# Attention stage: where the rounds of a top-k, a broadcast and the weight loads stand in their engines' orders

## The chip, the cores and the metric

The kernel runs on one core of one Trainium2 chip. The metric is the device time of one execution in microseconds. A core has five engines that run their own instruction queues in order: TensorE (PE: matmuls, and PEld for the loads of their weights), VectorE (DVE), ScalarE (ACT), GpSimd (POOL) and SyncE (SP), which here only issues DMAs. Weights and data come from HBM to SBUF by DMA; matmul results land in PSUM, in banks of 512 floats per partition.

## The reference: one step of a two-layer encoder

The input is 512 new frames of one stream ("prompt") and 64 further frames of another ("sample"), 576 tokens in all, of width 1024. Layer 0 mixes tokens with causal pooling, layer 1 with sparse attention; each layer then has an MLP of width 4096 with squared ReLU, and RMS norms stand before each part and at the end. The change touches layer 1's attention:

```python
p = h @ w_in                       # q (16 heads x 64), k, v (4 x 64), qi (8 x 64), ki (64), wi (8)
q, k, qi, ki = rope(q), rope(k), rope(qi), rope(ki)
logits = einsum('bthd,bsd->bths', qi, kidx) * 64 ** -0.5
score  = einsum('bths,bth->bts', relu(logits), wi)          # the indexer
score  = where(kpos // 64 <= qpos // 64, score, NEG)
_, idx = top_k(score, n_sel)                                # 128 of 512, 144 of 576
s = (q . k[idx]) * 64 ** -0.5                               # only the selected keys
o = softmax(s) @ v[idx];  y = o @ w_o
```

All arithmetic is in 32 bits. The kernel keeps each operand as a rounded part and a rest and adds three products, so that one block of weights means three times the matmuls.

## The kernel before, in words

Data lie transposed, features on the 128 partitions and the 576 tokens along the free axis (the prompt's 512, then the sample's 64). Weights come in blocks of 128x1024 floats. `load` takes a raw buffer (`raw_tile`, line 139) and issues the DMA, on ScalarE's queue for the attention's weights and on SyncE's for most of the MLP's; `split_block` (line 200) makes the rounded part on ScalarE (line 205) and the rest on VectorE (line 206) or GpSimd; three split blocks (`BLOCKS`) and two raw buffers (`RAWS`) exist. `loaded` (line 246) issues loads in the order of a list of jobs; `LOADS_AHEAD` says how many raw blocks may be held beyond the one that is being split: four where the stage has the extra raw buffers named `more`, one in the attention stage. `next_block` keeps `AHEAD`, two, split blocks ready.

The program is traced through a scheduler which, against a simulated timeline, chooses the order of each engine's instructions: of what is ready then, what was traced first goes first. The order is fixed before the run. `tc.manual_schedule(engines=...)` leaves the named engines' instructions in the order in which they are written; the kernel has two such places, outside the attention. `tc.issue_after(instruction)` keeps what is traced under it behind that instruction in its engine's order; `mixing` uses it for SyncE.

The attention stage, `attention` (line 1086), goes like this.

1. Two blocks of the indexer's queries, tokens 128 to 575, are projected (`project_qi`, line 1102, tile `pi`). Behind the first, `norm.stats` sums squares by matmul (tile `st`) and makes each token's factor `r` on VectorE (lines 394 to 401). `norm.spread` (line 350) then puts `r` on diagonals (lines 365 and 368), multiplies them by ones on TensorE (tile `rb`, line 355), so that each partition gets the factors of all tokens, and copies the two halves on ScalarE (line 356). With them the cosine table (GpSimd, line 1115) and the sine table (VectorE, line 1116) are scaled.
2. The block of the indexer's key and weights is projected (`ki`), and `rope` (line 1126) applies the tables. For the key, copies and products are done in two halves of 288 tokens (lines 1184 to 1190). The indexer's weights are transposed into the bank `pw` (line 1191), which comes from the pool `ps` (two tiles of two banks), and scaled (line 1195). The pool `po` has four tiles of one bank.
3. k, q and v are projected (tiles `pj` and `v`); the queries go through HBM (`qd`). Between the steps of these projections, `pace` (line 1421) puts `index_scores` (line 1211) of row blocks 1 to 3: 128 query tokens each, against i + 1 blocks of 128 keys. Row block 4 is the sample: 64 queries, 576 keys.
4. `top_k` (line 1247) works in place on a row block's scores `work[i]`: 16 rounds (18 in block 4), each of which finds the eight largest of each row (line 1253) and replaces them with a mark (line 1254). A last step (line 1257) makes a mask of it. All on VectorE.
5. `steps` (line 1394) runs 40 units of attention, each two heads (four for the sample) of one key head and one row block: units 0 to 15 take blocks 0 and 1 in turn, 16 to 23 block 2, 24 to 31 block 3, 32 to 39 block 4. A unit has scores on TensorE (`sc`, lines 1289 and 1297), a masked reduction on VectorE (line 1268, with the row's extreme `nm`), an exponential on ScalarE (line 1269), transposes on TensorE (`pt`, line 1309), a copy (line 1310) and the product with the values (`o`, line 1328). `top_k(i)` is traced ahead of the first unit of block i.
6. From unit 18 on, a first part of the output projection (`wa`, line 1383) goes between the units, and the rest (`wo`) behind them.

Of the kernel before, what the change touches and what calls it, by code (L numbers as in the profile page):

```python
# [16 lines left out]
P = 128  # L17
# [23 lines left out]
LOADS_AHEAD = {True: 4, False: 1}  # L41
# [4 lines left out]
STATS = (3, 0)  # L46
BLOCKS = 3
# [4 lines left out]
def pool_dsa_kernel(ctx: ExitStack, tc: tile.TileContext, a, o):  # L52
# [86 lines left out]
    def raw_tile(mlp=False):  # L139
        more = False  # L140
        if mlp and "more" in phase:
            t, turns["raw"] = turns["raw"], turns["raw"] + 1
            more = t % 4 > 1
        return (phase["more"] if more else raws).tile([P, 4 * 264], F32, tag="raw", name=uid("raw"))

    def load(src, n, queue, mlp=False):
        raw = raw_tile(mlp)
        d = queue.dma_start(raw[:, :n], src)
        if queue is nc.sync:
            last_of["sync"] = d  # L150
        return raw
# [94 lines left out]
    def loaded():  # L246

        waiting, held = [], 0
        while jobs or waiting:
            while jobs and held < LOADS_AHEAD["more" in phase] and ("last" in phase or jobs[0][0] not in ("pair", "made")):  # L250
# [67 lines left out]
    def project(pt, w, xs, between=iter(()), cols=((0, HT), (HT, HT)), ks=range(KT)):  # L318

        for k in ks:  # L320
            next(between, None)
            wh, wl = at(w, k)
            for i, (wt, part) in enumerate(((wh, 0), (wh, 1), (wl, 0))):
                for h, (c, m) in enumerate(cols):
                    pe.matmul(  # L325
                        pt[h][:, :m] if isinstance(pt, tuple) else pt[:, h, :m], wt, xs[k][:, part, c:c + m],
                        start=(k == ks[0] and i == 0), stop=(k == ks[-1] and i == 2),
# [758 lines left out]
    def attention(parts):  # L1086
# [15 lines left out]
        def project_qi():  # L1102
            pt = psum1("pi")
            project((pt,), next_block(), xs, cols=((P, T - P),))
            return pt[:, :T - P]

        q0 = [project_qi()]
        norm.stats()
        r = norm.r
        q0.append(project_qi())  # L1110
        two = psum("rb")
        rb = norm.spread((two[:, 0], two[:, 1]))
        pki = psum("ki")
        project(pki, next_block(), xs)
        pool.tensor_tensor(cs, cs, rb, ALU.mult)
        dve.tensor_tensor(sn, sn, rb, ALU.mult)
        def split_cache(src, s, new, sub=dve):
# [3 lines left out]
            raw = raw_tile()  # L1121
# [62 lines left out]
        for h in range(2):  # L1184
            at = slice(h * HT, (h + 1) * HT)
            act.copy(wt[0:32, at], pki[0:32, h, :HT])
            for to, c, table in ((t1, 96, cs), (t2, 64, sn)):
                for i in range(2):
                    rows = slice(c, c + 32) if i == 0 else slice(160 - c, 192 - c)
                    dve.tensor_tensor(to[32 * i:32 * i + 32, at], pki[rows, h, :HT], table[rows, at], ALU.mult)  # L1190
        pw = psum("pw")[:, 0]
# [55 lines left out]
        def top_k(i):  # L1247
# [3 lines left out]
            for _ in range(16 if i < 4 else 18):  # L1251
                m8 = small(8, "m8")
                dve.max(m8[:np_], wk[:np_])  # L1253
# [333 lines left out]
```

## Time and profile before

| | |
|---|---|
| median of 3 runs | 1120.38 us (1119.23 to 1123.69) |
| the profiled execution | 1120.8 us |
| its span | 1119.0 us |
| mean granted TensorE clock | 0.986 |
| the attention stage in the trace | 433 us to some 726 us |
| DMA, whole span | 183.54 MB, 164 GB/s |

Times in the trace count from the start of the span. A row of the timeline has start, duration, engine, line, operation, output and inputs, shapes and count; in brackets stands how long the engine had been idle and what released it. A row of waits has the waiting engine and its line, whom it waited for, the total in us, how often, and the longest. A round of the top-k shows as MAX8, MATCH_VALUE_LOAD and MATCH_REPLACE8. Rows of MAX8 can be told apart by their width: 256, 384 and 512 for row blocks 1 to 3, 64x576 for block 4.

### The profile page before, as it was taken

How to read it: one execution, taken by the hardware profiler on the slowest of the kernel's cores; microseconds unless marked ns; L12 is line 12 of the kernel's file. 1: busy time of each engine (PE TensorE's matmuls, PEld its weight loads, DVE VectorE, ACT ScalarE, POOL GpSimd, SP SyncE). 2: the span in 40 equal slices, each digit the busy share in tenths (PEclk: the TensorE clock that was granted, in tenths of full speed). 3: DMA queues.
4: the chain of work that ended last, by engine and by line, in shares of the span. 5: the costliest groups of instructions: out<-in, count | busy, mean ns of one | idle time of the engine just before them, and what ended most of it. 6: DMA issues, size and time to landing. Idle time of an engine off the chain costs nothing.

```text
span 1119.0 us, 20356 instructions
## 1 busy us (share of the span) xinstructions
PE 1083.9 (97%) x8027; PEld 1064.5 (95%) x8027; DVE 798.4 (71%) x1445; ACT 557.5 (50%) x940; POOL 296.5 (26%) x227
## 2 busy tenths in 40 slices
PE   9999999999999999999789999999999999999996
PEld 8999999999999989899778999999999999999995
DVE  7767656756755887789988963778757867865644
ACT  8544344334434454354358665655536636644542
POOL 3014504532451560287815342001000000000002
PEclk9999999999999999999969999999999999999998
DMA  6265489479568977476622333357576655545402
GB/s 221 70 192 139 140 237 272 122 203 274 154 163 254 241 185 227 116 217 169 177 86 57 108 98 108 109 174 211 166 227 179 194 169 162 162 160 171 142 19 85
DMA packets 81263, 183.54 MB, mean 164 GB/s; under 512 B 11809, under 2 KB 23376, under 8 KB 81168
## 3 DMA queue, kind: packets, MB, share of 16 engines
q1 hardware_dynamic: 64512, 143.94, 39.7%
q0 software_dynamic: 13056, 25.17, 13.6%
q10 hardware_dynamic: 3600, 13.14, 3.8%
q8 instruction: 63, 1.03, 0.4%
q14 instruction: 32, 0.26, 0.1%
HBM read 167.14 MB, written 61.22 MB: 204 GB/s over the span
## 4 chain that ended last, share of the span: by engine, by line
PE 72%; DVE 13%; DMA 5%; ACT 3%; POOL 3%; issue 3%; SPq 0%; DVEq 0%; ACTq 0%; POOLq 0%
PE up L586 17%; PE seed L428 15%; PE c L428 10%; PE a L428 10%; PE dn L325 4%; DVE w L206 4%; PE wo L325 2%; PE o L1328 2%; DMA mixed<-mixed 2%; DVE work L1254 2%; DVE m L1253 2%; PE wa L325 2%; PE pb L1053 1%; PE pi L325 1%; PE sc L1289 1%
## 5 line engine op out<-in xcount | busy, mean ns | idle before, releaser
L205 ACT CAST w<-raw 128x1024 fp32r<-128x1024 f32 (+2 forms) x242 | 211.2, 890 | 210.1 <-PE seed L428 80.5
L206 DVE TENSOR_TENSOR w<-raw,w 128x1024 fp32r<-128x1024 f32 (+2 forms) x224 | 249.1, 1119 | 50.0 <-ACT w L205 49.3
L586 PE MATMUL up<-xs,w 128*128 128x288 f32 x1536 | 206.3, 295 | 0.0
L586 PEld LDWEIGHTS up<-xs,w 128*128 128x128 f32 x1536 | 204.0, 188 | 0.2
L428 PE MATMUL seed<-u,w 128*128 128x288 f32 x1008 | 146.4, 296 | 3.0 <-ACT seed L447 1.4
L428 PEld LDWEIGHTS seed<-u,w 128*128 128x128 f32 x1008 | 138.1, 188 | 4.3 <-ACT seed L447 1.6
L428 PE MATMUL c<-u,w 128*128 128x288 f32 x672 | 100.8, 297 | 2.0 <-DVE w L206 1.2
L428 PE MATMUL a<-u,w 128*128 128x288 f32 x672 | 100.0, 295 | 1.5 <-ACT w L205 1.2
L428 PEld LDWEIGHTS c<-u,w 128*128 128x128 f32 x672 | 93.2, 188 | 3.2 <-DVE w L206 1.7
L428 PEld LDWEIGHTS a<-u,w 128*128 128x128 f32 x672 | 93.0, 188 | 2.3 <-ACT w L205 1.7
L811 POOL TENSOR_TENSOR x<-x,spare 128x320 f32<-128x320 f32 (+1 forms) x9 | 8.2, 946 | 233.3 <-ACT spare L807 233.3
L325 PE MATMUL pj<-xs,w 128*128 128x288 f32 x480 | 67.3, 295 | 2.3 <-DVE wi L1195 1.0
L325 PEld LDWEIGHTS pj<-xs,w 128*128 128x128 f32 x480 | 65.0, 188 | 3.7 <-issue 2.5
L235 POOL DMA_DIRECT2D mixed<-in_w_down x24 | 27.6, 1271 | 145.3 <-DMA mixed<-mixed 94.2
L235 POOL DMA_DIRECT2D mixed<-in_w_up x24 | 28.0, 1210 | 141.6 <-DMA mixed<-mixed 100.4
L428 PE MATMUL seed<-bx,w 128*128 128x288 f32 x432 | 62.5, 296 | 0.0
L428 PEld LDWEIGHTS seed<-bx,w 128*128 128x128 f32 x432 | 59.3, 188 | 0.1
L206 DVE TENSOR_TENSOR w<-sum,w 128x1024 fp32r<-128x1024 f32 (+1 forms) x32 | 34.6, 1080 | 34.5 <-ACT w L205 34.5
L284 POOL TENSOR_TENSOR sum<-raw 128x512 f32<-128x512 f32 x16 | 24.2, 1516 | 125.1 <-DMA raw<-in_w_down 125.1
L721 DVE SCALAR_TENSOR_TENSOR v<-up,rbm 128x288 f32<-128x288 f32 x80 | 32.6, 450 | 31.8 <-PE up L586 28.9
L205 ACT CAST w<-sum 128x1024 fp32r<-128x1024 f32 (+1 forms) x32 | 26.7, 834 | 56.6 <-POOL sum L289 45.2
L1269 ACT ACTIVATE p<-p,nm 128x128 f32<-128x128 f32 (+4 forms) x72 | 41.8, 582 | 20.2 <-DVE nm L1268 20.0
(298 smaller groups left out, 2047.8 us busy)
## 6 DMA issues: line engine op xcount, KB each, us to landing
raw<-in_w_up SPq DMA_DIRECT2D x52, 512.0 KB, 4.5
raw<-in_w_down SPq DMA_DIRECT2D x52, 512.0 KB, 4.4
raw<-mixed SPq DMA_DIRECT2D x48, 512.0 KB, 4.1
mixed<-in_w_down POOLq DMA_DIRECT2D x24, 512.0 KB, 8.3
mixed<-mixed SPq DMA_DIRECT2D x24, 512.0 KB, 8.2
mixed<-in_w_up POOLq DMA_DIRECT2D x24, 512.0 KB, 10.3
raw<-in_w_in ACTq DMA_DIRECT2D x15, 512.0 KB, 4.5
mixed<-in_w_down SPq DMA_DIRECT2D x12, 512.0 KB, 7.3
```

Source lines behind the costliest of these rows:

```text
L205: act.copy(w[:, 0, at], src[:, at])
L206: how["sub"].tensor_tensor(w[:, 1, at], src[:, at], f32(w[:, 0, at]), ALU.subtract)
L235: pool.dma_start(to, add, accum_op=ALU.add)
L284: pool.tensor_tensor(s[:, :512], r2[:, :512], r2[:, 512:], ALU.add)
L325: pe.matmul(pt[h][:, :m] if isinstance(pt, tuple) else pt[:, h, :m], wt, xs[k][:, part, c:c + m], start=(k == ks[0] and i == 0), stop=(k = ...
L428: pe.matmul(bank[:, :HT], wt[:, at], ut, start=first and j == 0 and i == 0, stop=j == 3 and i == 2, skip_group_check=True)
L586: pe.matmul(pt[h][:, :HT], w[:, wt, k * P:(k + 1) * P], moving(k, part, h), start=n == 0 and i == 0, stop=n == KT - 1 and i == 2)
L721: dve.scalar_tensor_tensor(v[:, 2 * i + h], pt[h][:, :HT], 0.0, halves(norm.rb)[:, h], ALU.max, ALU.mult)
L1253: dve.max(m8[:np_], wk[:np_])
L1254: dve.match_replace(wk[:np_], m8[:np_], wk[:np_], TAKEN)
L1269: act.activation(dst, dst, AF.Exp, scale=-1.0, bias=nm, accum_out=sums)
L1328: pe.matmul(oc[:, 2 * s + hh], pT[:, c:c + P], V[:, kt, vs], start=kt == 0, stop=kt == i)
```

## The change

It has five parts, all in the attention stage.

- `HELD` holds a round of the top-k and so all later rounds of its block, since each works on what the one before left: round 10 of block 2 is issued behind unit 1's last masked reduction, round 0 of block 3 behind unit 3's, round 0 of block 4 behind unit 9's.
- TensorE's instructions from the first `project_qi` to the key block are left in written order, and `norm.spread` stands amid the second block: behind six of its eight steps.
- A third raw buffer of 1024 columns, which every third load of at most 1024 columns takes; two raw blocks are held ahead rather than one.
- The copy and the products of the indexer's key take both halves in one instruction.
- The bank `pw` comes from the pool `po`.

```diff
+HELD = {(2, 10): 1, (3, 0): 3, (4, 0): 9}
...
+    def raw_tile(mlp=False, n=4 * 264):
+        for name, every in (("more", 4), ("third", 3)):
+            if name in phase and (mlp or name == "third" and n <= 1024):
+                turns["raw"] += 1
+                if turns["raw"] % every > 1:
+                    return phase[name].tile([P, 4 * 264 if name == "more" else 1024], F32, tag="raw", name=uid("raw"))
+        return raws.tile([P, 4 * 264], F32, tag="raw", name=uid("raw"))
...
-            while jobs and held < LOADS_AHEAD["more" in phase] and ("last" in phase or jobs[0][0] not in ("pair", "made")):
+            while jobs and held < (4 if "more" in phase else 2 if "third" in phase else 1) and ("last" in phase or jobs[0][0] not in ("pair", "made")):
...
-        def project_qi():
+        def project_qi(amid=None):
             pt = psum1("pi")
-            project((pt,), next_block(), xs, cols=((P, T - P),))
+            w = next_block()
+            for ks in (range(KT - 2), range(KT - 2, KT)) if amid else (range(KT),):
+                if ks[0]:
+                    amid()
+                project((pt,), w, xs, cols=((P, T - P),), ks=ks, ends=(0, KT - 1))
             return pt[:, :T - P]
 
-        q0 = [project_qi()]
-        norm.stats()
-        r = norm.r
-        q0.append(project_qi())
-        two = psum("rb")
-        rb = norm.spread((two[:, 0], two[:, 1]))
-        pki = psum("ki")
-        project(pki, next_block(), xs)
+        with tc.manual_schedule(engines={ENG.PE}):
+            q0 = [project_qi()]
+            norm.stats()
+            r = norm.r
+            two = psum("rb")
+            q0.append(project_qi(lambda: norm.spread((two[:, 0], two[:, 1]))))
+            rb = norm.rb
+            pki = psum("ki")
+            project(pki, next_block(), xs)
...
-        for h in range(2):
-            at = slice(h * HT, (h + 1) * HT)
-            act.copy(wt[0:32, at], pki[0:32, h, :HT])
-            for to, c, table in ((t1, 96, cs), (t2, 64, sn)):
-                for i in range(2):
-                    rows = slice(c, c + 32) if i == 0 else slice(160 - c, 192 - c)
-                    dve.tensor_tensor(to[32 * i:32 * i + 32, at], pki[rows, h, :HT], table[rows, at], ALU.mult)
-        pw = psum("pw")[:, 0]
+        act.copy(halves(wt[0:32]), pki[0:32, :, :HT])
+        for to, first, table in ((t1, 96, cs), (t2, 64, sn)):
+            for i, c in enumerate((first, 160 - first)):
+                dve.tensor_tensor(halves(to[32 * i:32 * i + 32]), pki[c:c + 32, :, :HT], halves(table[c:c + 32]), ALU.mult)
+        pw = psum1("pw")
...
-            for _ in range(16 if i < 4 else 18):
+            for n in range(16 if i < 4 else 18):
                 m8 = small(8, "m8")
-                dve.max(m8[:np_], wk[:np_])
+                behind = HELD.get((i, n))
+                with tc.issue_after(units[behind].softmax.ins) if behind else nullcontext():
+                    dve.max(m8[:np_], wk[:np_])
...
-    with stage(under=1, xs=1, slots=1, cst1=1, tmps=5, cst2=1), ExitStack() as parts:
+    with stage(under=1, xs=1, slots=1, cst1=1, tmps=5, cst2=1, third=1), ExitStack() as parts:
```

`softmax` now returns its reduction, which each unit keeps as `self.softmax`; `project` takes `ends`, the steps at which a bank's sum begins and ends, so that one sum can be written in two calls.

More of the change, by code (lines that the diff above doesn't have):

```diff
@@ L1 @@
-from contextlib import ExitStack, contextmanager
+from contextlib import ExitStack, contextmanager, nullcontext
 import numpy as np
@@ L40 @@
 RAWS = 2
-LOADS_AHEAD = {True: 4, False: 1}
 FACTORS = ("b11", "b22", "b21", "t3", "t1", "t2", "t4")
@@ L137, in pool_dsa_kernel @@
     last_of = {}
[L139 to L144, printed above, removed]
+    def raw_tile(mlp=False, n=4 * 264):
[5 more added lines that the diff above has]
+        return raws.tile([P, 4 * 264], F32, tag="raw", name=uid("raw"))
     def load(src, n, queue, mlp=False):
-        raw = raw_tile(mlp)
+        raw = raw_tile(mlp, n)
         d = queue.dma_start(raw[:, :n], src)
@@ L316, in split, with project @@
             dve.scalar_tensor_tensor(dst[:, 1], src, scale, f32(dst[:, 0]), ALU.mult, ALU.subtract)
-    def project(pt, w, xs, between=iter(()), cols=((0, HT), (HT, HT)), ks=range(KT)):
+    def project(pt, w, xs, between=iter(()), cols=((0, HT), (HT, HT)), ks=range(KT), ends=None):
         for k in ks:
@@ L326, in project @@
                         pt[h][:, :m] if isinstance(pt, tuple) else pt[:, h, :m], wt, xs[k][:, part, c:c + m],
-                        start=(k == ks[0] and i == 0), stop=(k == ks[-1] and i == 2),
+                        start=(k == (ends or ks)[0] and i == 0), stop=(k == (ends or ks)[-1] and i == 2),
                     )
@@ L1120, in split_cache @@
             dve.tensor_copy(t[:, :, TP:], f32(new[:, :, TP:]))
-            raw = raw_tile()
+            raw = raw_tile(n=TP)
             nc.sync.dma_start(raw[:, :TP], src)
@@ L1267, in softmax @@
             nm = small(1, "nm")
-            dve.tensor_tensor_reduce(dst, src, mask, -0.125, 3e38, ALU.add, ALU.min, nm)
+            d = dve.tensor_tensor_reduce(dst, src, mask, -0.125, 3e38, ALU.add, ALU.min, nm)
             act.activation(dst, dst, AF.Exp, scale=-1.0, bias=nm, accum_out=sums)
+            return d
         class Unit:
@@ L1290, in scores @@
                     for hh in range(2):
-                        softmax(pt[:, hh, :n], mask, self.pr[:, hh], self.group.sums[:, 2 * s + hh:2 * s + hh + 1])
+                        self.softmax = softmax(pt[:, hh, :n], mask, self.pr[:, hh], self.group.sums[:, 2 * s + hh:2 * s + hh + 1])
                 else:
@@ L1297, in scores @@
                             pe.matmul(pt[:, c, :HT], q[:, s], self.group.ck[:, part, c * HT:(c + 1) * HT], start=part == 0, stop=part == 1)
-                    softmax(pt[:, :, :HT], halves(mask), halves(self.pr), self.group.sums[:, s:s + 1])
+                    self.softmax = softmax(pt[:, :, :HT], halves(mask), halves(self.pr), self.group.sums[:, s:s + 1])
             def transpose(self):
```

## The prediction, made before the changed kernel was timed

> **What bounds the kernel now.** The page comes first: the span of the profiled execution, the engines, the clock.
>
> ```profile
> span 1119.0 us, 20356 instructions
> PE 1083.9 (97%) x8027; PEld 1064.5 (95%) x8027; DVE 798.4 (71%) x1445; ACT 557.5 (50%) x940; POOL 296.5 (26%) x227
> ```
>
> TensorE is busy 97% of the span, so nothing off it counts unless it makes TensorE wait or run slowly: only 35 us of idle time are to be had in the whole kernel. The change touches the attention stage alone. Therefore the view of busy time by stretch, over that stage (columns: time, length, then busy time and instructions of PE, PEld, DVE, ACT, POOL, the granted clock, DMA share, GB/s):
>
> ```profile
> 433.00:463.00 30.00, 29.06 (x165) 26.68 (x164) 18.19 (x37) 10.23 (x20) 5.20 (x5) 1.00 0.35 108
> 463.00:480.00 17.00, 15.64 (x110) 14.61 (x111) 13.98 (x25) 8.59 (x18) 4.25 (x3) 1.00 0.67 191
> 480.00:554.00 74.00, 72.53 (x545) 71.16 (x544) 68.50 (x144) 32.84 (x65) 61.85 (x39) 1.00 0.68 181
> 554.00:561.60 7.60, 0.94 (x8) 0.80 (x8) 7.46 (x23) 1.36 (x5) 2.71 (x2) 0.62 0.86 245
> 561.60:566.30 4.70, 4.66 (x22) 4.26 (x23) 3.95 (x17) 3.44 (x15) 0.00 (x0) 0.52 0.60 212
> 566.30:576.50 10.20, 8.05 (x61) 6.89 (x60) 10.10 (x38) 5.43 (x21) 0.00 (x0) 0.99 0.29 77
> 576.50:586.80 10.30, 10.30 (x52) 10.20 (x51) 6.95 (x26) 6.34 (x22) 3.68 (x3) 0.51 0.10 26
> 586.80:606.00 19.20, 17.46 (x144) 16.43 (x142) 14.44 (x62) 16.95 (x57) 15.31 (x12) 1.00 0.21 57
> 606.00:666.00 60.00, 59.62 (x486) 57.48 (x485) 49.47 (x138) 40.50 (x94) 20.40 (x18) 1.00 0.31 93
> ```
>
> Three things stand out. From 554 to 561.6 TensorE does 0.94 us of work while VectorE is full (7.46 of 7.60). The clock then is at half until 566.3 and again from 576.5 to 586.8, and TensorE works through both: 22 matmuls in 4.66 us, 52 in 10.30 us, against 61 in 8.05 us between them at full clock. From 606 on there is nothing to gain. The view of waits says who was waited for over the stage:
>
> ```profile
> PE pt L1309 <- ACT p L1269: 7.8, 5, 6.7
> PE o L1328 <- DVE ot L1373: 1.5, 1, 1.5
> PE pj L325 <- DVE wi L1195: 1.0, 1, 1.0
> PE pj L325 <- DVE t L1190: 0.9, 1, 0.9
> PE v L1454 <- DVE w L206: 0.9, 1, 0.9
> PE pj L325 <- ACT rp L1144: 0.4, 1, 0.4
> ```
>
> One wait of 6.7 us is the hole. The timeline shows that ScalarE, which it names, is only the messenger:
>
> ```profile
> 543.62 0.56 DVE L1253 MAX8 m<-work 128x8 f32<-128x384 f32 x1
> 553.84 1.11 PE L1289 MATMUL sc<-k,q 128*128 128x128 f32 x8 [0.56 <-ACT V L1456]
> 560.14 0.69 DVE L1253 MAX8 m<-work 128x8 f32<-128x512 f32 x1
> 560.74 0.27 DVE L1268 CUSTOM_DVE_ANT_0 p<-sc,mask 128x128 f32<-128x128 f32 x1
> 561.06 0.40 ACT L1269 ACTIVATE p<-p,nm 128x128 f32<-128x128 f32 x1 [6.24 <-DVE nm L1268]
> 561.60 0.47 PE L1309 MATMUL pt<-ident,p 128*128 128x128 f32 x1 [6.66 <-ACT p L1269]
> ```
>
> The scores of units 0 and 1 are finished at 554.95 (553.84 + 1.11), but their first reduction starts on VectorE at 560.74: rounds of the top-k of row blocks 2 (384 wide) and 3 (512 wide) stand ahead of it in VectorE's order.
>
> **The holds.** Round 10 of block 2 (the row at 543.62) and all that follows must now come behind unit 1's reductions, round 0 of block 3 behind unit 3's, round 0 of block 4 behind unit 9's. What moves is the rounds' busy time (the maxima of line 1253, then the match loads and replacements of line 1254) between 543.6 and 560.7; the third row is all of VectorE after that, to the end of block 4's mask:
>
> ```profile
> 543.60:560.70 17.10, 6.59 (x11) 0.86 0.69 205
> 543.60:560.70 17.10, 6.61 (x20) 0.86 0.69 205
> 560.70:654.80 94.10, 88.89 (x663) 84.47 (x663) 81.47 (x271) 65.86 (x192) 34.61 (x30) 0.92 0.28 84
> 654.33 0.42 DVE L1257 TENSOR_SCALAR work<-work 64x576 f32<-64x576 f32 x1
> 666.05 0.76 DVE L1268 CUSTOM_DVE_ANT_0 p<-sc,work 128x576 f32<-128x576 f32 x1 [2.82 <-PE sc L1297]
> ```
>
> So 6.59 + 6.61 = 13.2 us of rounds go from before the first softmax to behind it.
>
> What that gives. From the reduction's start to the transpose it takes 561.60 - 560.74 = 0.86 us; with about 0.2 us from the scores' end to the reduction (an estimate; the transpose starts 0.14 us after its exponential ends, 561.06 + 0.40 to 561.60), 1.1 us of the 6.66 stay. Gain 5.5 us; bounds 0 (something else stands ahead of the reduction) and 5.8.
>
> The clock is next. It falls to half in the hole (0.62 on the mean of that stretch) and stays there to 566.3. Without the hole that first drop should not come, and the 4.66 us done at 0.52 would take about half. I take 2.0 us, bounds 0 and 2.3. The second slow stretch has its own cause: the second wait above, 1.5 us, comes shortly ahead of it, amid a row of small units:
>
> ```profile
> 573.83 0.66 PE L1328 MATMUL o<-V,pT 128*128 128x64 f32 x4 [1.54 <-DVE ot L1373]
> ```
>
> The change removes no cause of it that I can name, so I count nothing; its bounds are 0 and 5.0 us (10.30 at 0.51), and a drop at another place costs the same 5.
>
> What is late next. Behind each held round's wait stands only VectorE's own order; the wait is an order, not a stall, and what had filled VectorE before 554 becomes idle time there. The rounds must fit later. From 555.2 VectorE has 81.47 + 13.2 = 94.7 us to do until block 4's mask, so that is ready at 649.9 at the earliest; with all of the idle time that it had from 560.7 (94.10 - 81.47 = 12.6 us), at 662.5. It was ready at 654.8 and first used at 666.05; with TensorE 7.5 us ahead it is wanted at 658.5. So 8.6 of the 12.6 us of idleness may remain at no cost; if all of it remains, 4.0 us are lost. Masks 2 and 3 have far more room: unit 16 and unit 24, which read them, begin when 16 and 24 units are through. The rounds can also delay a reduction by their length, as the 1.5 us wait for line 1373 is today. I give back 1.5 us, nearer to the lower end of 0 to 4.0, because part of that idleness (10.30 - 6.95 = 3.4 us) lies in a stretch where TensorE itself was slow.
>
> **The broadcast amid the second block, and TensorE's written order.** These rows of the timeline, and one of line 1190's instructions, price it:
>
> ```profile
> 439.33 7.23 PE L325 MATMUL pi<-xs,w 128*128 128x448 f32 x34
> 441.86 0.25 DVE L368 TENSOR_SCALAR diag<-ident,r 128x64 f32<-128x64 f32 x1
> 450.88 0.40 ACT L356 COPY rba<-rb 128x288 f32<-128x288 f32 x1 [3.39 <-PE rb L355]
> 451.36 2.00 POOL L1115 TENSOR_TENSOR cs<-cs,rba 128x576 f32<-128x576 f32 x1 [18.12 <-ACT rba L356]
> 453.39 0.62 DVE L1139 TENSOR_TENSOR rp<-pi,cs 128x448 f32<-128x448 f32 x1 [1.32 <-POOL cs L1115]
> 464.01 0.74 DVE L1196 TENSOR_TENSOR ki<-t,t 32x576 f32<-32x576 f32 x1
> L1190 DVE TENSOR_TENSOR t<-ki,cs x4: 453/456/460, 455.6 to 461.4; 32x288 f32<-32x288 f32 x4
> ```
>
> Today 34 matmuls, ten of them of the third block, run before the broadcast, and its second half comes amid the key block. Now it stands behind 18 matmuls of the second: 439.33 + 18 x 7.23/34 = 443.2, with the diagonal ready at 442.1. TensorE issues the same instructions, so it gains nothing by the order itself; if VectorE puts another pair of splits ahead of the diagonal, the margin of 1.05 us is about used up (bounds 0 and +1; I take 0). The copies then end near 445 rather than at 451.3, and the cosine product on GpSimd and the rotary work on VectorE start some 6 us sooner. VectorE is 18.19 of 30 busy there, so this fits.
>
> What TensorE gets of it is the waits for PSUM: 0.9 us for line 1190 (the key bank is read in halves, the last of them after 461.4) and 1.0 us for line 1195 (the small bank of the indexer weights sits in the pool of large banks, which it leaves now). Both should go: 1.9 us, bounds 0 and 2.3 with the 0.4 for line 1144. Merging the halves makes four products of some 0.74 us (the nearest row, line 1196, 32x576) of eight of 0.456, 0.7 us less on VectorE, hidden by its idleness; the merged copy likewise.
>
> **The third raw buffer, two loads ahead.** The same loads, earlier. TensorE's waits above hold none for a transfer; only the 0.9 us for a split of the value block (line 1454) is of this family, and VectorE's queue is as much its cause. I take 0.4 us for everything that VectorE does sooner; bounds 0 and 0.9. Its cost, a load issued before its buffer is free, would hold up ScalarE, which issues the loads; with one buffer more that is less likely than today.
>
> **The sum.** Against the profiled execution's 1120.8 us (span 1119.0 and 1.8 around it): -5.5 - 2.0 + 1.5 - 1.9 - 0.4 = -8.3, so 1112.5. The median shown, 1120.38, is 0.4 below that execution; I predict 1112.
>
> **Rivals.** (A) VectorE takes it back. The hole closes, but the rounds find no room: 4.0 us are lost to block 4's mask and each of two more reductions is delayed by one round (1.4 us). 8.3 - 2.5 (the rest of the 4.0) - 2.8 leaves 3 us: 1117. For it: VectorE is 10.10 of 10.20 full at 566 to 576, where moved rounds would go. Against it: 3.4 us free right behind. If the hold merely exchanges what stands ahead of the first reduction, the result is the same or nearer to 1119.
>
> (B) The second slow stretch goes too, since its cause, a reduction late behind rounds, vanishes with VectorE's lag: 5.0 more and the 1.5 not given back, 1106. Against it: the same small units with as many rounds between them.
>
> (C) The clock stays down among the small units whatever they wait for. The rows speak for it: the second stretch was entered after 1.5 us of idleness only, and TensorE was 10.30 of 10.30 busy throughout it. Then one slow stretch of some 10 us with full work (5.0 us) stands in place of the first: 8.3 - 2.0 - 5.0 leaves 1.3, and up to 5 where that stretch falls on waits that TensorE has anyway; in the middle, 1117. The Trainium skill (TensorE: Matmul & The Clock Gate, Part 4: PE-mode transpose) says that transposes do not count as busy for the gate in the way that matmuls do, and these units are half transposes; its table in "Why this matters for your kernels" allows idle gaps up to about 3 us. By the second rule alone the first drop goes and the second would not exist; this trace shows the second at gaps of half that, so it agrees with the first rule rather than with the second.
>
> (D) Slower. The held rounds are put directly ahead of reductions for which TensorE waits, unit after unit, since the order is made before the run and VectorE runs behind it (today by 5.8 us at 560.74). If all 13.2 us of moved rounds stand so, they cost 13.2 against 8.3 + 1.5 = 9.8 gained, and the idleness keeps the clock down for one stretch more (5.0): 1120.4 + 13.2 - 9.8 + 5.0 = 1129. It decides from the point where more than 9.8 us of rounds, eight of the eleven, lie on TensorE's path. Against it: reductions come ahead of later top-k work in the program, so that a ready one goes first.
>
> **Chances.** Forecast 0.47, A 0.18, B 0.12, C 0.13, D 0.10. This measurement can tell 0.5%, 5.6 us, from no change: faster means under 1114.8, slower over 1126. The forecast (own range 1109 to 1115) lies below 1114.8 nine times in ten, B always, A and C one time in six: 0.42 + 0.12 + 0.05, say 0.61. Slower 0.11, same 0.28. The range reaches from B to A and C: 1105 to 1119.5.
>
> **What would show it.** The wait of line 1309 for line 1269 falls from 6.7 us to about 1; no round from the eleventh on of block 2 stands before the first reduction; clock 1.00 right behind the value projection; the broadcast's copies near 445; the waits for lines 1190 and 1195 gone; block 4's mask ready a few us before its first use. I am wrong if the transpose still waits over 3 us, if a new slow stretch appears between 556 and 600, or if reductions wait behind rounds so that units 8 to 31 are no earlier than today.

## The result, and the profile after

| | us | runs |
|---|---|---|
| before, median | 1120.71 (1119.23 to 1124.69) | 7 |
| changed, median | 1115.93 (1112.88 to 1119.65) | 7 |
| ratio | 0.9949, 95% interval 0.9928 to 0.9971 | |
| profiled execution, before and changed | 1120.8 and 1115.93 | spans 1119.0 and 1114.2 |

The changed kernel is about 5 us faster: 5.7 us by the ratio, 4.8 by the medians. The forecast was 8.3 us and 1112. Its own range, 1109 to 1115, misses the median by 0.9; the whole range, 1105 to 1119.5, holds it. A time under 1114.8 had been given a chance of 0.61, and did not come. The profile and the experiments show a gain of about the size forecast or more, and beside it a loss that the prediction did not know of.

The page first. TensorE's work is what it was (1082.3 against 1083.9 us); what moved is its idle and slow time.

```profile
span 1114.2 us, 20339 instructions
PE 1082.3 (97%) x8027; PEld 1064.7 (96%) x8027; DVE 791.3 (71%) x1441; ACT 556.4 (50%) x939; POOL 295.2 (26%) x227
```

Busy time by stretch of the changed kernel, columns as in the prediction; the last row is VectorE's whole way from the first reduction to the first use of block 4's mask:

```profile
433.00:463.00 30.00, 25.52 (x138) 23.45 (x138) 16.56 (x35) 10.97 (x22) 4.47 (x5) 0.89 0.42 140
463.00:480.00 17.00, 17.00 (x101) 15.53 (x100) 13.98 (x25) 7.11 (x13) 3.17 (x3) 1.00 0.63 181
554.00:561.60 7.60, 6.88 (x58) 6.48 (x56) 2.03 (x7) 4.97 (x10) 6.12 (x5) 1.00 0.35 92
561.60:566.30 4.70, 4.21 (x32) 3.60 (x32) 4.67 (x25) 4.47 (x19) 1.79 (x2) 1.00 1.01 343
566.30:576.50 10.20, 7.33 (x45) 7.08 (x43) 5.91 (x27) 4.31 (x18) 0.00 (x0) 0.69 0.45 133
576.50:586.80 10.30, 10.03 (x84) 9.65 (x83) 10.15 (x39) 8.57 (x29) 6.97 (x6) 0.98 0.22 57
561.03:665.61 104.58, 99.63 (x794) 95.67 (x794) 98.01 (x319) 74.55 (x212) 41.84 (x35) 0.97 0.35 103
```

From 554 to 561.6 TensorE now does 58 matmuls instead of 8, at full clock. Most of them are still the value projection's, which ends at 559.77 (553.28 before), so it is the timeline below, and not this row, that shows the hole gone. But there are two places that the kernel before did not have: 4.5 us of idle time and a clock of 0.89 in the first row (before: 29.06 busy at 1.00), and a clock of 0.69 from 566.3 on. The view of waits of the stage names both:

```profile
PE seed L429 <- DVE x L490: 3.3, 1, 3.3
PE sc L1295 <- DMA q<-q: 2.9, 1, 2.9
PE pt L1315 <- ACT p L1274: 1.3, 4, 0.5
PE pw L1197 <- ACT wt L1190: 0.7, 1, 0.7
```

The 6.7 us for `p` became 0.5 at the longest. The waits for lines 1190 and 1195 of before are gone. New are 2.9 us for the load of a unit's queries, and 3.3 us for an addition at the end of the first MLP, ahead of the attention stage. The timeline where the hole was, and on to the wait for the queries:

```profile
560.33 1.11 PE L1295 MATMUL sc<-k,q 128*128 128x128 f32 x8 [0.56 <-ACT V L1462]
561.03 0.29 DVE L1273 CUSTOM_DVE_ANT_0 p<-sc,mask 128x128 f32<-128x128 f32 x1 [0.50 <-PE sc L1295]
561.91 0.56 DVE L1258 MAX8 m<-work 128x8 f32<-128x384 f32 x1
561.92 0.33 PE L1315 MATMUL pt<-ident,p 128*128 128x128 f32 x1 [0.47 <-ACT p L1274]
571.23 0.98 PE L1295 MATMUL sc<-k,q 128*128 128x256 f32 x3 [2.88 <-DMA q<-q]
```

VectorE has been idle when the first scores come, takes them at once, and the held round (MAX8, 384 wide) comes behind. The stall that ends at 571.23 is unit 6's: it has lasted 2.88 us, and by the trace's clock record the clock is at half from 570.1, within the stall, to 577.0.

And the timeline at the end of the first MLP:

```profile
419.97 0.35 ACTq L149 DMA_DIRECT2D raw<-in_w_in  x1
430.14 0.33 ACTq L149 DMA_DIRECT2D raw<-in_w_in  x1
436.12 0.62 ACT L206 CAST w<-raw 128x512 fp32r<-128x512 f32 x1 [5.08 <-DMA raw<-in_w_in]
436.77 0.69 DVE L207 TENSOR_TENSOR w<-raw,w 128x512 fp32r<-128x512 f32 x1 [2.96 <-ACT w L206]
437.38 0.45 DVE L490 TENSOR_TENSOR x<-x,seed 128x288 f32<-128x288 f32 x1
437.88 3.25 PE L429 MATMUL seed<-u,w 128*128 128x288 f32 x12 [3.28 <-DVE x L490]
```

The same in the timeline of the kernel before:

```profile
416.23 0.38 ACTq L148 DMA_DIRECT2D raw<-in_w_in  x1
416.75 0.34 ACTq L148 DMA_DIRECT2D raw<-in_w_in  x1
431.69 1.87 PE L428 MATMUL seed<-u,w 128*128 128x288 f32 x12 [0.79 <-DVE x L489]
```

Before, the attention's first two weight loads are issued together at 416. Now the second is issued at 430.14; its split on ScalarE waits 5.08 us for it, the split's second half on VectorE stands in the order ahead of the addition, and TensorE's last twelve `seed` matmuls wait 3.28 us for that addition and then run at half speed (3.25 us against 1.87; the clock record has half speed from 437.0 to 443.9). Nothing there waits for what the diff does in the attention. It comes from `raw_tile`, which the MLPs use too: the old one read the counter and then raised it (`t % 4 > 1`), the new one raises it first and then reads. So every raw buffer of the first MLP is dealt out one step earlier, and at its end one ordinary raw buffer is free instead of two. The second MLP's deal is moved too, and there the third buffer's loads, which raise the same counter, add to it. The text of the change calls all its parts parts of the attention stage, and so did the prediction.

### The profile page after: what moved, and what is told of

It reads as the page before. It is cut to its first block, busy times and chain, and to the rows that moved or that the text cites. A ratio compares the mean times of both kernels' runs of the same rounds, so it can differ in the third digit from the quotient of the medians.

```text
span 1114.2 us, 20339 instructions
## 1 busy us (share of the span) xinstructions
PE 1082.3 (97%) x8027; PEld 1064.7 (96%) x8027; DVE 791.3 (71%) x1441; ACT 556.4 (50%) x939; POOL 295.2 (26%) x227
## 4 chain that ended last, share of the span: by engine, by line
PE 73%; DVE 7%; DMA 7%; POOL 5%; issue 4%; ACT 3%; SPq 0%; DVEq 0%; POOLq 0%; ACTq 0%
PE seed L429 14%; PE up L587 13%; PE c L429 9%; PE a L429 9%; PE pj L326 6%; PE dn L326 4%; PE o L1334 3%; DVE w L207 2%; DMA raw<-in_w_down 2%; PE wa L326 2%; PE pi L326 2%; DMA mixed<-mixed 2%; PE sc L1295 1%; PE z L949 1%; PE pt L1315 1%
## 5 line engine op out<-in xcount | busy, mean ns | idle before, releaser
L587 PE MATMUL up<-bx,w 128*128 128x288 f32 x288 | 51.0, 295 | 0.7 <-DVE x L1481 0.7
```

The lines of the kernel that those rows point to most:

```text
L587: pe.matmul(pt[h][:, :HT], w[:, wt, k * P:(k + 1) * P], moving(k, part, h), start=n == 0 and i == 0, stop=n == KT - 1 and i == 2)
```

## The experiments

All ratios are to the kernel before, run on the same chip in the same job, with a 95% interval. Kernels of different jobs are compared by these ratios. Medians in us.

| | edit | median | ratio |
|---|---|---|---|
| the change | all of it | 1115.93 | 0.9949 (0.9928 to 0.9971) |
| e1 | before + shifted count | 1119.91 | 0.9987 (0.9968 to 1.0006) |
| e2 | before + third buffer, two ahead | 1123.09 | 1.0013 (0.9989 to 1.0036) |
| e3 | before + holds | 1114.50 | 0.9932 (0.9907 to 0.9957) |
| e4 | before + written order, broadcast, merged key, `pw` | 1121.03 | 1.0001 (0.9979 to 1.0023) |
| e5 | before again, one profile | 1120.38 | |
| e6 | e3 + a fourth query buffer | 1111.81 | 0.9924 (0.9901 to 0.9946) |
| e7 | change, old count, no third buffer, one ahead | 1109.01 | 0.9903 (0.9879 to 0.9926) |
| e8 | change, old count, third buffer's loads later | 1109.21 | 0.9905 (0.9878 to 0.9931) |
| e9 | change, old count | 1111.56 | 0.9908 (0.9884 to 0.9931) |
| e10 | change, third buffer's loads later | 1113.52 | 0.9927 (0.9900 to 0.9954) |
| e11 | e7 + stores of the values on GpSimd's queue | 1113.60 | 0.9925 (0.9901 to 0.9949) |
| e12 | e7 with nine more rounds held | 1119.44 | 0.9979 (0.9955 to 1.0003) |

### One part at a time: e1 to e4

e1 puts only the new count into the kernel before; the third buffer's branch is never taken.

```diff
-            t, turns["raw"] = turns["raw"], turns["raw"] + 1
-            more = t % 4 > 1
+                turns["raw"] += 1
+                if turns["raw"] % every > 1:
```

> The kernel before with one thing of the change alone: the counter that deals the raw blocks of the MLPs out to their two pairs of buffers is raised before it is read, so that the pattern of two and two is shifted by one block. Nothing else differs. Theory 1 (the change has costs outside the attention stage that the prediction did not see, and this is one): the last block of the first MLP then leaves only one of two raw buffers free, the second block of the attention's weights comes late, and its split stands in VectorE's order ahead of the addition for which TensorE waits. So TensorE waits some 3 us at the end of the first MLP (3.3 in the changed kernel, 0.8 before) and loses 1 to 3 us more to the clock: 3 to 7 us slower than before, 1124 to 1127. Rival (that hole comes from the new order of the attention stage or from the third buffer): within 1.5 us of before, and the wait stays near 0.8.

e2 puts only the third raw buffer in, with the old count, and two raw blocks ahead.

```diff
+                if (turns["raw"] - (name == "more")) % every > 1:
...
-            while jobs and held < LOADS_AHEAD["more" in phase] and ("last" in phase or jobs[0][0] not in ("pair", "made")):
+            while jobs and held < (4 if "more" in phase else 2 if "third" in phase else 1) and ("last" in phase or jobs[0][0] not in ("pair", "made")):
...
+    with stage(under=1, xs=1, slots=1, cst1=1, tmps=5, cst2=1, third=1), ExitStack() as parts:
```

> The kernel before with the third raw buffer and two loads ahead alone; the pattern of the MLPs' buffers in the first MLP is as before. Theory 1: the buffer lies in memory that is free from the start, so its first load is ScalarE's first instruction and takes DMA time from the loads of x: the first matmul of tile z comes 1.4 us later than before (9.1 for 7.7) and the stage behind it 1.5 to 2.6 later; no hole at the end of the first MLP. The buffer itself gains under 1 us in the attention stage: 1120 to 1123. Rival (the late start of the changed kernel was chance, the buffer does good in the stage): first z at 7.7, 1117 to 1120.

e3 puts only the holds in.

```diff
+HELD = {(2, 10): 1, (3, 0): 3, (4, 0): 9}
...
+                with tc.issue_after(units[behind].softmax.ins) if behind else nullcontext():
```

> The kernel before with the holds alone. Theory 1: the holds give more than the whole change does, since the other parts cost: the wait of the first transpose for its exponential falls from 6.7 to about 1 us, no slow stretch of the clock between 554 and 567, and the units end 7 to 11 us earlier: 1109 to 1113. Rival (VectorE takes back half of it, so that the holds give just what the change gave): 1114 to 1117.

e4 puts only the written order, the broadcast amid the second block, the merged instructions of the key and the bank of `pw` in.

```diff
+        with tc.manual_schedule(engines={ENG.PE}):
+            q0 = [project_qi()]
...
+            q0.append(project_qi(lambda: norm.spread((two[:, 0], two[:, 1]))))
...
+        pw = psum1("pw")
```

> The kernel before with TensorE's written order, the broadcast amid the second block, the merged products of the indexer's key and the small bank in the other pool; no holds, no third buffer. Theory 1: the waits for lines 1190 and 1195 go (1.9 us) and nothing is lost: 1118 to 1120, the hole at 554 to 561 unchanged. Rival (the order costs: the broadcast's second half waits for the copy of the first, 0.5 us, and the first transpose of the indexer's weights for its copy, 0.7 us, and the last block of queries comes late by as much as in the changed kernel, 3 us): 1121 to 1124.

Waits of e1 (from 425 us to 554 us), then of e2, e3 and e4, each from its own view:

```profile
PE seed L429 <- DVE x L490: 3.0, 1, 3.0
```

```profile
PE pj L326 <- DVE t L1191: 3.8, 1, 3.8
```

```profile
PE sc L1293 <- DMA q<-q: 2.9, 1, 2.9
PE pt L1313 <- ACT p L1272: 1.6, 5, 0.6
```

```profile
PE ix L1227 <- DVE kis L1209: 1.3, 1, 1.3
PE pj L326 <- ACT w L206: 0.8, 1, 0.8
PE pt L1318 <- ACT p L1277: 9.1, 2, 8.7
```

What follows. The holds carry the gain: 0.9932 alone, 7.6 us (4.8 to 10.4 by the interval), and with them alone the hole closes and the wait for the queries (2.9 us) appears; so that wait is the holds' doing, not that of the third buffer. The count alone brings the 3.0 us wait for the addition, as in the changed kernel, so a cause of that wait is shown (not the only one: e6 below has it without the count); yet alone it costs nothing that can be measured (0.9987). The third buffer alone shows no gain (1.0013): the loads run two ahead, their splits stand on VectorE ahead of the key's products, and the wait for these grows from 0.9 to 3.8 us. The written order alone shows no gain (1.0001, with 2.4 us either way by the interval): the waits that it removes come back as others, 1.3 us for `kis`, 0.8 for a split, and the hole grows from 6.7 to 8.7 us. From the first `pi` to the last `v` it takes 121.5 us in e4's profile, no less than before's 119.9, so TensorE was not sooner at the hole either.

By the medians the expectations of e1 (3 to 7 us slower), e3 (1109 to 1113) and e4 (1118 to 1120) were missed; e3 and e4 came out in their rivals' ranges.

### The second profile of before: e5

> The kernel before again, unchanged, for a second profile: what of the differences between two profiles is chance. Theory 1 (the shifted pattern and the third buffer cost time at places of their own): the first matmul of tile z is again near 7.7, the last addition of the first MLP makes TensorE wait 0.8, and the clock has slow stretches of some 10 us near 556 and 576 again. Rival (the clock's stretches and the start vary by themselves, and the profile of before had more slow time among the units than is usual): first z anywhere from 7.7 to 9, and at 576 no slow stretch.

Busy time by stretch in it, the same stretches as the prediction's:

```profile
554.00:561.60 7.60, 3.06 (x25) 2.66 (x23) 7.39 (x20) 3.12 (x7) 4.75 (x4) 1.00 0.87 251
561.60:566.30 4.70, 2.01 (x9) 1.61 (x9) 3.94 (x18) 2.04 (x10) 0.00 (x0) 0.51 0.66 202
576.50:586.80 10.30, 9.76 (x67) 9.26 (x68) 9.06 (x37) 8.08 (x28) 3.54 (x3) 0.83 0.17 46
```

The hole is there again, but the slow stretches are not what they were: 6.8 us and 3.4 us (from 561.7 and 578.8 on) against 10.2 and 10.2. The prediction priced the clock's part by one execution; the second would have made it smaller. The execution's time is nearly the same, 1120.38, because its first part, up to the first `pi` matmul, is 3.4 us longer. The clock record has two slow stretches of 3.4 us in that part, from 19.0 and 391.0 us on, and none there in the first profile; at half clock the two cost as much as the difference.

### What takes part of the gain: e6 to e11

e6 gives the queries a fourth buffer beside the holds alone.

```diff
-        return phase["xs" if tag == "xs" else "slots"].tile([P, n], dt, tag=tag, bufs=SLOTS[tag], name=uid(s))
+        return phase["xs" if tag == "xs" else "slots"].tile([P, n], dt, tag=tag, bufs=4 if tag == "a" and "cst2" in phase else SLOTS[tag], name=uid(s))
```

> The kernel before with the holds, and four buffers rather than three for the units' queries (tile q). With the holds alone the scores of one unit waited 2.9 us for the load of their queries, which stands in SyncE's queue behind the stores of the values and finds a free buffer only when an earlier unit is through. Theory 1 (that wait is the next thing that is late, and it brings the clock's short slow stretch at 568 with it): the wait goes, 2 to 5 us faster than the holds alone, 1109 to 1112. Rival (VectorE, which has all the rounds still to do, is the limit behind it, so the wait only moves there): within 1 us of the holds alone, 1113 to 1115.5.

e7 is the changed kernel with the old count and without the third buffer; e8 is the changed kernel with the old count, where the loads on ScalarE's queue in the attention stage stand behind the first MLP's norm.

```diff
-                if turns["raw"] % every > 1:
+                if (turns["raw"] - (name == "more")) % every > 1:
...
-    with stage(under=1, xs=1, slots=1, cst1=1, tmps=5, cst2=1, third=1), ExitStack() as parts:
+    with stage(under=1, xs=1, slots=1, cst1=1, tmps=5, cst2=1), ExitStack() as parts:
```

> The changed kernel without the third raw buffer, with one load ahead, and with the MLPs' pattern of buffers as before: the holds, TensorE's written order, the merged key and the small bank stay. Theory 1 (the third buffer and what comes with it cost the change some 2 us): 1112 to 1115, level with the holds alone or a little better. Rival (the third buffer does no harm in company, since the merged key takes away the wait that it brought when alone): as the changed kernel, 1115 to 1117.

```diff
-                if turns["raw"] % every > 1:
+                if (turns["raw"] - (name == "more")) % every > 1:
...
-        d = queue.dma_start(raw[:, :n], src)
+        behind = last_of.get("norm") if queue is act and "third" in phase else None
+        with tc.issue_after(behind.ins) if behind else nullcontext():
+            d = queue.dma_start(raw[:, :n], src)
...
+        last_of["norm"] = last_of["rt"]
```

> The changed kernel with the MLPs' pattern of buffers as before and with the third buffer's loads held behind the first MLP's norm on ScalarE, so that none of them is issued at the kernel's start; all else as in the change. Theory 1 (the early load costs 1 to 2.5 us at the start, the shifted pattern some at the first MLP's end): first matmul of z near 8, no wait of 3 us at the end of the first MLP, 1112 to 1114.5. Rival (both are covered or chance): as the changed kernel, 1115 to 1117.

e9 has only the old count (the first line pair of e8's diff), e10 only the later loads (the rest of it).

> The changed kernel with the MLPs' pattern of buffers as before; the third buffer's first load is still ScalarE's first instruction. It differs from the kernel with that load held in that alone. Theory 1 (the early load costs by itself): first matmul of z near 9 rather than 8, 1 to 2.5 us slower than with the load held: 1110 to 1112. Rival 1 (the early load costs nothing, the shifted pattern all): 1108.5 to 1109.5. Rival 2 (the early load costs all of it): 1114 to 1117.

> The changed kernel with the third buffer's loads held behind the first MLP's norm, and the MLPs' pattern of buffers shifted as in the change. It differs from the changed kernel in the held load alone, and from the kernel of the earlier run with held loads in the pattern alone. Theory 1 (the shifted pattern costs in company, through the wait of some 3 us at the end of the first MLP and a slow stretch of the clock there): that wait is 3 us, 3 to 5 us slower than with the pattern as before: 1112 to 1115. Rival (as in the run with the pattern alone, it costs nothing in the end): 1108 to 1110.

e11 is e7 with the two stores of the values' output on another queue, since the query loads share SyncE's queue with them.

```diff
-        nc.sync.dma_start(o["v_p"], V[:, 0:4])
-        nc.sync.dma_start(o["v_s"], V[:TS, 8])
+        pool.dma_start(o["v_p"], V[:, 0:4])
+        pool.dma_start(o["v_s"], V[:TS, 8])
```

> The changed kernel without the third buffer and with the pattern as before, and with the two stores of the values issued by GpSimd rather than by SyncE, so that they no longer stand ahead of the loads of the units' queries. Theory 1 (those stores make unit 6's queries late, which costs 3.3 us there): the wait of the scores for a load of q falls below 1.5 us, 1 to 3 us faster than without: 1106 to 1108. Rival (the loads are late for the buffers or for the traffic, not for their place in the queue): wait and time as without, 1108.5 to 1110.

The waits of e9 (old count) and of e10 (shifted count) at the first MLP's end, each from its own view:

```profile
PE seed L429 <- DVE x L490: 0.8, 1, 0.8
```

```profile
PE seed L431 <- DVE x L492: 3.2, 1, 3.2
```

Why the third buffer's loads were tried later shows in the changed kernel's timeline at the very start:

```profile
0.75 0.38 ACTq L149 DMA_DIRECT2D raw<-in_w_in  x1
9.12 6.11 PE L949 MATMUL z<-w,xs 128*128 128x256 f32 x48 [1.42 <-ACT w L922]
```

The third buffer lies in memory that nothing uses earlier, so the scheduler makes its first load, by the order of the loads the attention's sixth weight block, whose split starts at 462.03 us, ScalarE's first instruction at 0.75 us; the first `z` matmul comes at 9.12 us (7.67 before). That the one makes the other late is not shown: the three kernels with the early load have the first `z` at 8.5 to 9.1 us, those without at 7.6 to 9.0 (9.02 in e11, which has no third buffer).

One more view tells the stages apart: the rows of TensorE's first indexer projection, of the last group of value matmuls (its end is start plus duration) and of the last of the output projection, from the timelines of the changed kernel and of e9.

```profile
440.92 6.37 PE L326 MATMUL pi<-xs,w 128*128 128x448 f32 x24
545.50 14.27 PE L1460 MATMUL v<-w,xs 128*128 128x256 f32 x120
704.80 16.84 PE L326 MATMUL wo<-ot,w 128*128 128x320 f32 x114
```

```profile
437.07 5.02 PE L326 MATMUL pi<-xs,w 128*128 128x448 f32 x24
544.78 9.79 PE L1460 MATMUL v<-w,xs 128*128 128x256 f32 x82
704.76 11.46 PE L326 MATMUL wo<-ot,w 128*128 128x320 f32 x77
```

Worked out from these rows and the same ones of the other kernels, in us:

| | start to first `pi` | to the last `v` | to the last `wo` | the last `wo` ends |
|---|---|---|---|---|
| before, first and second profile | 433.4, 436.8 | 119.9, 119.2 | 172.9, 169.8 | 726.2, 725.8 |
| e1, count alone | 439.3 | 120.9 | 165.5 | 725.7 |
| e2, third buffer alone | 439.5 | 123.6 | 165.7 | 728.8 |
| e4, order alone | 435.6 | 121.5 | 166.3 | 723.5 |
| e3, holds alone | 436.0 | 119.8 | 163.2 | 718.9 |
| e6 | 436.9 | 121.5 | 158.8 | 717.2 |
| the change | 440.9 | 118.9 | 161.9 | 721.7 |
| e7 | 435.6 | 117.6 | 161.7 | 714.8 |
| e8 | 435.1 | 117.6 | 160.8 | 713.5 |
| e9 | 437.1 | 117.5 | 161.7 | 716.2 |
| e10 | 437.7 | 118.4 | 161.6 | 717.7 |
| e11 | 436.5 | 117.6 | 163.9 | 717.9 |
| e12 | 437.3 | 117.6 | 175.7 | 730.6 |

Against the two profiles of before the softmax stage of the change is 7.9 to 11.0 us shorter, and the part before the attention 4.1 to 7.5 longer (it differs by 3.4 between the two). But the third column hangs on the first two. Without holds (before, e1, e2, e4) the last `wo` ends at 723.5 to 728.8 us, whether the last `v` ends at 553.3 or at 563.1: a late entry is made good, and the column falls to 165.5 without any hold. With the change's holds, alone or in company, the last `wo` ends at 713.5 to 721.7, in the main the earlier the sooner the values are done.

With the count back (e9), 3.8 us of the first column and 1.4 of the second come back and the third stays. That the 3.8 are the count's doing can't be read from these profiles: e10 keeps the shifted count and its wait, and has 437.7 there. The measured times say more. The old count alone takes the ratio from 0.9949 to 0.9908, 4.6 us; the intervals of the two just touch, and that of e7 (old count, no third buffer) lies clear of the change's. The later loads alone take it to 0.9927, 2.5 us, and both to 0.9905; the interval of e10 overlaps those of the change and of e8, so the price of the loads, and of the count once the loads stand later, is not clear of nothing. Between e8 and e9 there is no difference, so with the old count the early load costs nothing that these runs can tell. e9 puts back the first MLP's deal alone, since the third buffer's loads still move the second's; but nothing is gained there, as from the last `wo` to the end it takes 394.3 us in e9 and 392.6 in the change.

By the medians e7 and e8 were faster than either range that had been expected of them, and e11's time lies in neither of its two.

The wait for the queries is not settled. A fourth buffer removes it (e6). e8 has it neither, without such a buffer, but its first transposes wait 2.3 us for `p` instead, and a slow stretch of 6.8 us follows from 557.4 on. Another queue for the stores does not remove it (e11: 3.2 us again, and no gain, 0.9925 against e7's 0.9903, intervals that overlap). So it was not those stores. Whether it is the buffer's being freed late or the traffic at that moment (the stretch from 561.6 has 343 GB/s and a DMA share of 1.01), the runs don't say. In e6 the fourth buffer also moved other tiles, and the wait of 3.0 us at the first MLP's end appeared without the shifted count, which may be why e6 gained no more over e3 than 0.9924 against 0.9932; no run shows it.

### The limit of the holds: e12

e12 is e7 with round 1 of block 2 in place of round 10 behind unit 1: nine more rounds, of some 1.1 us each (0.56 for the maxima, 0.54 for the replacement), go from before the softmaxes to amid them.

```diff
-HELD = {(2, 10): 1, (3, 0): 3, (4, 0): 9}
+HELD = {(2, 1): 1, (3, 0): 3, (4, 0): 9}
```

> The changed kernel without the third buffer and with the pattern as before, and with row block 2 held from round 1 rather than round 10: nine more rounds, 10.7 us by the rounds' rows, are moved behind unit 1. Theory 1 (VectorE has no room left: block 4's mask is ready just when unit 32 reads it): that mask comes 6 to 11 us later and TensorE, once it has done its other work, waits for it: 3 to 9 us slower, 1112 to 1118. Rival (there is room, since other work of VectorE moves ahead): within 1.5 us, 1107.5 to 1110.5.

The timeline of the changed kernel, where block 4's mask is made and first used:

```profile
665.13 0.45 DVE L1262 TENSOR_SCALAR work<-work 64x576 f32<-64x576 f32 x1
665.61 0.76 DVE L1273 CUSTOM_DVE_ANT_0 p<-sc,work 128x576 f32<-128x576 f32 x1
```

Busy time, waits and timeline of e12 in its turn:

```profile
555.00:673.00 118.00, 108.64 (x853) 102.84 (x853) 109.48 (x352) 78.15 (x218) 46.73 (x40) 0.97 0.33 99
```

```profile
PE pt L1315 <- ACT p L1274: 5.2, 8, 1.7
PE o L1338 <- ACT pT L1321: 2.5, 1, 2.5
```

```profile
672.30 0.44 DVE L1262 TENSOR_SCALAR work<-work 64x576 f32<-64x576 f32 x1
672.77 0.76 DVE L1273 CUSTOM_DVE_ANT_0 p<-sc,work 128x576 f32<-128x576 f32 x1
```

Already in the changed kernel the reduction of unit 32 follows the mask without a gap (665.13 + 0.45, then 665.61). With 9.9 us more of rounds there, the mask is made and the reduction starts at 672.77, 14.5 us after e7's (658.26; 1.7 of it is a later start of the stage). The waits for `p` go from 2.2 to 5.2 us, and the kernel loses 8.5 us by the ratios (0.9979 against 0.9903). The profiled execution is the slowest of e12's twelve (1125.57, median 1119.44), so its own loss is larger than that. What the holds gained is given back nearly whole: VectorE sets the pace there. How many rounds fit between the two holds no run shows.

## Why the prediction was right, and where it was not

- **The holds: mechanism right, size not told apart.** The sum gave the softmax stage 5.5 + 2.0 - 1.5 = 6.0 us. Alone the holds gave 7.6 (e3), and the interval, 4.8 to 10.4, holds both. The wait fell to 0.47, not 1.1: VectorE is idle and takes the first scores at 561.03, while the last of the eight score matmuls ends at 561.44 (560.33 + 1.11), where the working had VectorE start only behind them all. The term for the clock, 2.0, was made from one execution; in the second profile of before the stretches were shorter (e5).
- **The second slow stretch.** It was counted as unchanged. A slow stretch from 570.1 to 577.0 began within the new wait of 2.9 us for the queries. "A new slow stretch between 556 and 600" was one of the things that were to show the prediction wrong; it came, out of a load that no step named. What was late next after the hole was not VectorE but the queries.
- **VectorE's room.** "Ready a few us before its first use" is wrong: the mask has no slack left, where the working expected that some of the 12.6 us of idleness would be used up. VectorE is 98.01 of 104.58 busy. In the change that shows in no wait of TensorE for `p` above 0.5 us, since TensorE had other units' work to do meanwhile; e12 shows what it costs a step further: a row of waits for `p`, and 8.5 us.
- **The written order and the broadcast.** The 1.9 us were to come from two waits, which did go; 1.0 of it, the wait for line 1195, was 0.2 in the second profile of before. Alone the part showed no gain (e4, 1.0001), though the interval doesn't exclude 1.9. In company of the holds its stretch, from the first `pi` to the last `v`, is some 2 us shorter (117.5 or 117.6 in e7, e8, e9, e11 and e12, against 119.8 in e3 and 119.9 and 119.2 before), so by the profiles the size was about right with the holds beside it. In the times it is not clear: e7 at 0.9903 against e3 at 0.9932, with intervals that overlap. The copies near 445 did not come so; the timeline of the changed kernel has the second half of the broadcast and its copy here:

```profile
453.13 0.75 PE L356 MATMUL rb<-diag,ones 128*128 128x288 f32 x2 [0.49 <-ACT rba L357]
453.92 0.40 ACT L357 COPY rba<-rb 128x288 f32<-128x288 f32 x1 [0.84 <-PE rb L356]
```

  The copy ends 13.4 us after the first `pi` matmul (454.32 - 440.92), against 17.9 before and 11.6 expected; the rest of the difference is the late start.
- **The third buffer, "the same loads, earlier".** The 0.4 us are too little for these intervals, and nothing speaks for them: alone 1.0013 (e2), and e7, which lacks it, is as fast as e8. Its near-neutral price stands, its reason only half: the loads are earlier, but so are the splits, ahead of the key's products (3.8 us in e2), and the first load goes to the kernel's start.
- **The rivals.** C, a clock that stays down among the small units whatever they wait for, falls: from 576.5 to 586.8 TensorE does 84 matmuls in 10.03 us at 0.98, where before it was 52 at 0.51, and in e6, where the queries are not late, the clock record has no slow stretch among the units at all. The rule that was cited for it from the Trainium skill (TensorE: Matmul & The Clock Gate, Part 4: PE-mode transpose), that transposes don't count as busy in the way that matmuls do, doesn't keep the clock down in this stretch of the trace. But it is hardly put to the test: 18 of the 84 matmuls there (`pt` and `ot`) are transposes, not half as the prediction said. B's slow stretch did go from its old place, and another came at 570.1. What A describes came only with more rounds held (e12), and D's slowdown in no run. The three chances added up to 0.61 in the prediction make 0.59.
- **The step that failed: "The change touches the attention stage alone".** The count in `raw_tile` is shared with both MLPs, and raising it before reading shifts their buffers. The wait appears with the count and goes with it (e1, e9, e10), and e9 against the change puts the count's price at 4.6 us, or 1 to 8 if the two intervals are combined. Without it the change is at 0.9908, 10.3 us faster than before (7.7 to 13.0 by the interval), which holds the sum's 8.3; a loss that the sum didn't contain brought the time to just above the forecast's own range. That the whole range still holds it is partly luck: it reached up to 1119.5 for A and C, and neither is what happened.

What stays open: why the shifted count costs nothing by itself (0.9987) and some 4.6 us in company. In e1 the stage is entered 2.5 us later than in e5 (5.9 later than in the first profile), and against e5 4.5 us are made good between the first reductions of units 0 and 16 (567.59 to 599.39; 563.39 to 599.72 in e5). The last column of the table says much the same of the other kernels without holds. That fits a stage which VectorE sets as long as its backlog of rounds stands there, so that TensorE's delay is hidden, and doesn't once the holds have taken the backlog away. That it is the backlog is argued; no run takes it away by itself.

## What to carry to other kernels

A diff is read for every caller of the functions that it touches: a counter raised before instead of after its use moved the buffers of two stages that the change was not about, and the change without it was 4.6 us faster, about as much as it gave with it. When a stall is taken away, look for what had been hiding in it (here a load of queries 9 us further on), and ask how much room the engine that takes the moved work has left: here it had none. Parts are best tried in company too: the written order showed no gain alone, and by the profiles some 2 us once the holds were there. And a stage's length in one profile is read beside the time at which it was entered: without the holds a late start was made good.

## What the runs showed of the hardware

The granted clock varies from run to run of one and the same kernel. If a run's time below full clock is taken as time at half clock, it is twice (1 - mean clock) times the span; over 31 runs of before in one job that is 20 to 41 us, and the time rises with it by 0.33 us per us (0.33 and 0.28 in the other two jobs): 1117.85 us in the middle at a mean clock of 0.991, 1126.4 at 0.982 (five runs each, among the 59 of before in the three jobs). So a single execution of before can lie 8 us from another, as much as the difference that was to be forecast. And by the trace's clock record the slow stretches inside the kernel (the one that runs to its end aside) had few lengths, 3.4, 6.8 or 10.2 us, and came at waits as short as 1.5 us (before, where the wait ends at 573.83 and the stretch begins at 576.3) and 2.9 us (the change, 570.1). Much the same wait of some 3 us at the first MLP's end came with 6.8 us of half clock in the change and in e1, and with 3.4 in e6 and e10. Before another forecast of this size the clock term should be taken from several profiles.
